# Thirty arrangements of the same products in the up-projection of a feed-forward block

## The chip, the core and the metric

The kernel runs on one core of one Trainium2 chip. The metric is the device time of one execution in microseconds; the time of a kernel is the median of several executions on the same chip.

## The reference

One layer of a decoder works on 272 tokens (16 meta tokens and 256 of the sequence) of width 2048. First comes a sparse attention beside a causal pooling, then a feed-forward part. Only the feed-forward part matters here:

```python
def conv_gated_ffn(h, w_up, conv_w, conv_b, w_down):
    T = h.shape[1]
    z = h @ w_up
    zp = jnp.pad(z, ((0, 0), (CONV_WIDTH - 1, 0), (0, 0)))
    z = sum(zp[:, j:j + T] * conv_w[j] for j in range(CONV_WIDTH)) + conv_b
    a, g = jnp.split(z, 2, axis=-1)
    return (jax.nn.gelu(a) * g) @ w_down
```

The inner width is 5632 for each of `a` and `g`. Everything is float32.

## The kernel before, in words

**Two parts per number.** Each float32 operand x of a large product is split into an upper part (x rounded to the format that TensorE multiplies in one pass, fp32r) and a lower part (x minus the upper part). A product of W and A is then three matmuls: upper W by upper A, upper W by lower A, lower W by upper A. `product` (lines 196 to 204) writes them in this order for each of the 16 row tiles k of the contraction (2048 = 16 x 128), so a block of 128 output channels is 48 matmuls that accumulate in one PSUM tile `mm`. The weights are the stationary operand (128 columns), the activations the moving one (258 columns: the 256 tokens and the two before them that the convolution needs). In the trace these are the lines 202, 203 and 204 with `mm<-hp,whl`.

**Weights.** `fetch` (lines 148 to 163) brings a weight tile of 128 x 2048 from HBM on the queue of SP into `wraw`; ScalarE (ACT) then writes the upper part (line 162) and VectorE (DVE) the lower part (line 163), each in two halves of 1024 columns, into the tile `whl`. There are three buffers of each, and the weights are fetched two blocks ahead. `whl` is a little longer than two parts need (4224 words a partition), and a table `spots` sets at which byte offsets the two parts begin: (0, 80) for the up-projection, where the second figure counts from 8192 bytes. The activations `hp` lie in slots of 576 words, the upper part from word 6, the lower one from word 270.

**The order of work.** `ffn_plan` writes the feed-forward part out as a list. The 44 tiles of the inner width are cut into parts of 8, 8, 8, 8, 8 and 4. Each of the 44 has two up blocks (for `a` and `g`), which makes 88. While the up blocks of one part are computed, the down-projection of the part before it is threaded between them, one weight tile after one up block. The first part, 16 up blocks, has no down-projection beside it; the other 72 up blocks have one.

**The down-projection** uses a Strassen-like scheme with seven products instead of eight: `forms` makes sums of the gated activations on GpSimd (POOL) and splits them into upper and lower parts (tiles `gp` and `right`), and `seven` (lines 770 to 793) runs for each weight tile four products (kind A), three (kind B) or, in one place, eight (kind C). Here the gated activations are stationary, and the weights move, 512 columns at a time: lines 791, 792, 793 with `at<-whl,gp` or `at<-whl,right`. In the program order of TensorE an up block of 48 matmuls is followed by 12 or 9 of the down-projection (24 for kind C).

After an up block, ACT and DVE apply the convolution, `gate` the two halves, and the result goes to `forms`. [...]

Of the kernel before, what the change touches and what calls it, by code (L numbers as in the profile page):

```python
# [17 lines left out]
P = 128  # L18
# [5 lines left out]
NQ = T - Q0  # L24
KT = D // P
# [9 lines left out]
PARTS = (8, 8, 8, 8, 8, 4)  # L35
# [37 lines left out]
def places(a, b):  # L73


    return a // 4, (8192 + (b if b >= a else b + 256)) // 4


def ffn_plan():

    plan, f0 = [], 0
    for part, n in enumerate(PARTS):
        ups = [("up", f, half_) for f in range(f0, f0 + n) for half_ in range(2)]
        downs = []
        if part:
            downs = [(kind, part - 1, c, j) for c in range(2) if (part - 1, c) != PLAIN for kind in "AB"
                     for j in range(PARTS[part - 1] // 2)]
        u, d = len(ups), len(downs)
        while ups or downs:
            if ups and (len(downs) * u <= len(ups) * d or not downs):  # L90
                plan.append(ups.pop(0))
            else:
                plan.append(downs.pop(0))
        f0 += n
    return plan + [("C", *PLAIN, j) for j in range(PARTS[PLAIN[0]] // 2)]
# [3 lines left out]
def tile_layer(ctx, tc, xt, w_first, w_proj, w_uk, w_uv, w_pool, w_o, w_up, w_down, cols, rows, rel_bias, onehot, out):  # L99
    nc = tc.nc  # L100
# [21 lines left out]
    ps = small()  # L122
# [4 lines left out]
    stream = [w_proj[j] for j in range(8)] + [w_uk, w_uv] + [w_proj[j] for j in range(8, 24)]  # L127
    stream += [w_o[j] for j in range(KT)]
    plan = ffn_plan()
    kinds, spots = {}, {}  # L130
    for i in range(8):
        spots[i], spots[10 + i], spots[18 + i] = ACROSS, QUERIES[i % 2], POOLED[i]
    for i in range(26, len(stream)):
# [1 line left out]
    for item in plan:  # L135
        if item[0] == "up":
            spots[len(stream)] = ACROSS
            stream.append(w_up[item[2] * FT + item[1]])
        else:
            kinds[len(stream)] = item[0]  # L140
            stream.append(w_down[sum(PARTS[:item[1]]) + item[2] * (PARTS[item[1]] // 2) + item[3]])
# [20 lines left out]
            nc.scalar.activation(hl[:, 0, c], raw[:, c], AF.Copy)  # L162
            nc.vector.tensor_tensor(hl[:, 1, c], raw[:, c], hl[:, 0, c].bitcast(F32), op=ALU.subtract)  # L163

    def weight_tiles(places):
        raw = wp.tile([P, 2048], F32, tag="wraw", name="wraw")
        t = wp.tile([P, WSLOT], F32R, tag="whl", name="whl")
        u, l = places
        return raw, Pair(t[:, u:u + 2048], t[:, l:l + 2048])

    def emit(i):
        if i in ready:
            return
        if i == spare:
            raw = wp.tile([P, 2048], F32, tag="wraw", name="wraw")
            hl = sb.tile([P, 2, 2048], F32R, tag="y", name="whl_y")
        else:
            raw, hl = weight_tiles(places(*spots.get(i, (0, 0))))
        fetch(raw, hl, stream[i], kinds.get(i))
        if i >= len(stream) - PARTS[-1]:  # L180
            k = i - len(stream) + PARTS[-1]
            nc.scalar.activation(raw[:, LAST:], raw[:, LAST:], AF.Copy, accum_out=wsums[:, k:k + 1])
        ready[i] = hl
# [6 lines left out]
    def weights(ahead=2):  # L190
        i = state["use"]
        state["use"] += 1
        prefetch(i + 1 + ahead)
        return ready.pop(i)

    def product(ps, hl, m, act, lo, hi, ks=range(KT), width=P, k0=0, k1=KT):

        for n in range(k0, k1):
            k = ks[n]
            wh, wl = hl[:, 0, k * width:k * width + m], hl[:, 1, k * width:k * width + m]  # L200
            ah, al = act[k][:, 0, lo:hi], act[k][:, 1, lo:hi]
            nc.tensor.matmul(ps, wh, ah, start=n == 0, stop=False)  # L202
            nc.tensor.matmul(ps, wh, al, start=False, stop=False)  # L203
            nc.tensor.matmul(ps, wl, ah, start=False, stop=n == KT - 1)  # L204
# [536 lines left out]
    def two_parts(a, src):  # L741
        nc.scalar.activation(a[:, 0], src, AF.Copy)
        nc.vector.tensor_tensor(a[:, 1], src, a[:, 0].bitcast(F32), op=ALU.subtract)
        return a

    def slot():
        a = fp.tile([P, 2, NE], F32R, name="gp", tag="gp", bufs=19)
        return a[:, :, :2 * P].rearrange("p a (b c) -> p a b c", c=P)

    def forms(p, r, j):

        a11, a21, a12, a22 = r[:, 0, :P], r[:, 0, P:], r[:, 1, :P], r[:, 1, P:]
        s = fp.tile([P, 4 * P], F32, name="forms", bufs=1).rearrange("p (a b) -> p a b", b=P)
        nc.gpsimd.tensor_tensor(s[:, 0], a21, a22, op=ALU.add)
        nc.gpsimd.tensor_tensor(s[:, 2], s[:, 0], a11, op=ALU.subtract)
        nc.gpsimd.tensor_tensor(s[:, 1], a12, s[:, 2], op=ALU.subtract)
        nc.gpsimd.tensor_tensor(s[:, 3], a11, a21, op=ALU.subtract)  # L759
        left = two_parts(slot(), r[:, :, :P])  # L760
        mid = two_parts(slot(), s[:, :2])
        right = ring.tile([P, SLOT], F32R, tag="act", name="right")
        right = Pair(*(right[:, o:o + 2 * P].rearrange("p (b c) -> p b c", c=P) for o in (0, T)))
        right = two_parts(right, s[:, 2:])
        if p == PLAIN[0]:
            lone, i = two_parts(slot(), r[:, :, P:]), 1
        else:
            if j % 2 == 0:
                held["lone"] = slot()
            lone, i = held["lone"], j % 2  # L770
            two_parts(lone[:, :, i], a22)
        return {"P1": (left, 0), "P2": (left, 1), "P5": (mid, 0), "P3": (mid, 1), "P6": (right, 0),
                "P7": (right, 1), "P4": (lone, i), "a21": (lone, 0)}

    def seven(kind, part, c, j):

        hl = weights()
        n = PARTS[part] // 2
        names = {"A": (("P2", 2), ("P3", 3), ("P1", 0), ("P5", 1)), "B": (("P7", 1), ("P6", 0), ("P4", 2)),
                 "C": (("P1", 0, "c11"), ("P2", 2, "c11"), ("P1", 1, "c12"), ("P2", 3, "c12"),  # L780
                       ("a21", 0, "c21"), ("P4", 2, "c21"), ("a21", 1, "c22"), ("P4", 3, "c22"))}[kind]
        done = []
        for name, w, *to in names:
            a, i = pairs[part][j][name]
            to = (to or [name])[0]
            fresh, last = j == 0 and to not in done, j == n - 1 and (kind != "C" or to in done)
            if fresh:
                held[to] = small()
            done.append(to)
            ps, w = held[to], slice(512 * w, 512 * w + 512)  # L790
            nc.tensor.matmul(ps, a[:, 0, i], hl[:, 0, w], start=fresh, stop=False)  # L791
            nc.tensor.matmul(ps, a[:, 0, i], hl[:, 1, w], start=False, stop=False)  # L792
            nc.tensor.matmul(ps, a[:, 1, i], hl[:, 0, w], start=False, stop=last)  # L793
        if j < n - 1:
            return
        c11, c12, c21, c22 = (y2[:, i, w:w + 512] for i in range(2) for w in (512 * c, 1024 + 512 * c))

        def add(to, ps):
            nc.vector.scalar_tensor_tensor(to, to, 1.0 if part else ALPHA, ps, op0=ALU.mult, op1=ALU.add)  # L799

        if kind == "C":
            for to, name in ((c11, "c11"), (c12, "c12"), (c21, "c21"), (c22, "c22")):
                add(to, held[name])
        elif kind == "A":
            held["u"] = fp.tile([P, 512], F32, name="u", tag="u1", bufs=1, padded_shape=[P, 2 * NQ])
            nc.scalar.activation(held["u"], held["P1"], AF.Copy)
            held["v"] = fp.tile([P, 512], F32, name="v", tag="u2", bufs=1, padded_shape=[P, 2 * NQ])
            nc.scalar.activation(held["v"], held["P5"], AF.Copy)
            add(c11, held["P2"])
            add(c12, held["P3"])  # L810
            nc.gpsimd.dma_start(c11, held["u"], accum_op=ALU.add)
            nc.gpsimd.dma_start(c12, held["v"], accum_op=ALU.add)
        else:
            u, v = held["u"], held["v"]
            add(c22, v)
            nc.vector.tensor_tensor(u, u, held["P6"], op=ALU.add)
            nc.vector.tensor_tensor(v, u, held["P7"], op=ALU.add)
            add(c21, held["P4"])
            nc.gpsimd.dma_start(c12, u, accum_op=ALU.add)
            nc.gpsimd.dma_start(c21, v, accum_op=ALU.add)  # L820
            nc.gpsimd.dma_start(c22, v, accum_op=ALU.add)
# [4 lines left out]
    for item in plan:  # L826
# [5 lines left out]
        if half_ == 0:  # L832
            if f % 2 == 0:
                pair = fp.tile([P, 2, S], F32, name="za", tag="z0", bufs=3)
            both = []
        hl = weights()
        ps = big()
        if todo and f > FOLDED - 1 + half_:
# [15 lines left out]
                continue  # L854
            both = [conv(i * FT + f, i, unfold(both[i]), pair[:, f % 2]) for i in range(2)]
        else:
            product(ps[:, :NQ], hl, P, h_parts, 0, NQ)
            both.append(conv(half_ * FT + f, half_, ps, pair[:, f % 2]))
            if half_ == 0:
                continue  # L860
# [190 lines left out]
```

## Time and profile before

| | |
|---|---|
| median of 3 runs | 1038.33 us (1038.06 to 1038.5) |
| the profiled execution, its own time | 1039.8 us |
| its span, first to last instruction | 1038.0 us |
| granted TensorE clock | 0.998 |
| TensorE (PE) busy | 1025.3 us, 99% of the span, 7649 matmuls |
| weight loads (PEld) busy | 973.8 us, 94% |
| DVE busy | 886.1 us, 85% |
| ACT busy | 617.4 us, 59% |
| POOL busy | 209.3 us, 20% |
| moved by DMA | 250.80 MB, mean 242 GB/s |

The profiled execution lies 1.5 us above the median of the runs; 1.8 us of its time lie outside the span. A row of a group names the line of the kernel, the engine, the operation, the tile written and those read, the shape and the count; behind the bar stand the busy time in us, the mean length of one in ns, and how long the engine was idle just before them. A row of the timeline has the start in us, the length in us, and the same names. Matmuls are pipelined, so that the length of one (0.28 us for 258 columns) is more than twice the distance between the starts of two; what a matmul costs is that distance.

### The profile page before, as it was taken

What the parts mean: (1) busy time and instruction counts of PE and PEld (TensorE: products, weight loads), DVE (VectorE), ACT (ScalarE), POOL (GpSimd) and SP (SyncE); (2) the same over time, 40 slices, a digit from 0 to 9 for tenths busy, and PEclk for the clock granted to TensorE, in tenths of its full rate; (3) what the DMA queues carried; (4) which work ended last, traced back from release to release, by engine and by line L of the source; (5) the groups of instructions that cost most, each with busy time, mean ns of one, the idle gap of its engine ahead of it and who ended that gap; (6) DMA issues with size and microseconds to landing.
All of it is one profiled execution on the core that took longest, in us unless ns stands there. A gap on an engine that the chain in (4) does not pass through costs nothing.

```text
span 1038.0 us, 19165 instructions
## 1 busy us (share of the span) xinstructions
PE 1025.3 (99%) x7649; PEld 973.8 (94%) x7649; DVE 886.1 (85%) x1372; ACT 617.4 (59%) x994; POOL 209.3 (20%) x262
## 2 busy tenths in 40 slices
PE   9999999999999999999999999999999999999996
PEld 8998999999999999998999999999999999999985
DVE  6879468758779997898999999899998998999866
ACT  7566356645447765565566655656555656566654
POOL 1100014125345311211122011120111201110022
PEclk9999999999999999999999999999999999999999
DMA  9766543454552587898798787887878878898766
GB/s 326 259 216 236 194 156 109 152 188 167 191 196 85 200 233 248 261 301 257 260 299 293 283 283 271 287 284 274 286 269 288 276 277 278 269 306 274 277 203 152
DMA packets 59610, 250.80 MB, mean 242 GB/s; under 512 B 21718, under 2 KB 22400, under 8 KB 32384
## 3 DMA queue, kind: packets, MB, share of 16 engines
q1 hardware_dynamic: 34016, 229.37, 61.5%
q0 software_dynamic: 8320, 17.71, 8.9%
q10 hardware_dynamic: 17184, 2.49, 1.4%
q8 instruction: 60, 0.98, 0.4%
q14 instruction: 30, 0.25, 0.1%
HBM read 233.55 MB, written 3.16 MB: 228 GB/s over the span
## 4 chain that ended last, share of the span: by engine, by line
PE 82%; DVE 7%; issue 5%; DMA 4%; POOL 1%; ACT 1%; DVEq 0%; POOLq 0%; ACTq 0%
PE mm L204 20%; PE mm L203 20%; PE mm L202 20%; PE at L792 5%; PE at L793 5%; PE at L791 5%; DVE whl L163 3%; DMA wraw<-in_w_down 2%; DMA wraw<-in_w_up 1%; DMA y<-x 1%; DVE x L704 1%; ACT whl L162 1%; DVE hp L708 1%; PE mm L265 1%; PE mm L267 1%
## 5 line engine op out<-in xcount | busy, mean ns | idle before, releaser
L163 DVE TENSOR_TENSOR whl<-wraw,whl 128x1024 fp32r<-128x1024 f32 (+1 forms) x418 | 492.7, 1213 | 53.8 <-ACT whl L162 52.9
L162 ACT ACTIVATE whl<-wraw 128x1024 fp32r<-128x1024 f32 (+1 forms) x418 | 405.0, 1014 | 147.4 <-DVE wraw L158 39.6
L204 PE MATMUL mm<-hp,whl 128*128 128x258 f32 x1280 | 360.8, 282 | 0.0
L203 PE MATMUL mm<-hp,whl 128*128 128x258 f32 x1280 | 359.7, 281 | 0.0
L202 PE MATMUL mm<-hp,whl 128*128 128x258 f32 x1280 | 355.5, 278 | 0.0
L202 PEld LDWEIGHTS mm<-hp,whl 128*128 128x128 f32 x1280 | 240.7, 188 | 3.1
L203 PEld LDWEIGHTS mm<-hp,whl 128*128 128x128 f32 x1280 | 239.6, 187 | 3.0
L204 PEld LDWEIGHTS mm<-hp,whl 128*128 128x128 f32 x1280 | 240.2, 188 | 0.0
L202 PE MATMUL mm<-xp,whl 128*128 128x256 f32 (+5 forms) x384 | 110.9, 289 | 0.0
L203 PE MATMUL mm<-xp,whl 128*128 128x256 f32 (+5 forms) x384 | 108.5, 282 | 0.0
L204 PE MATMUL mm<-xp,whl 128*128 128x256 f32 (+5 forms) x384 | 108.1, 282 | 0.0
L791 PE MATMUL at<-whl,gp 128*128 128x512 f32 x212 | 83.8, 395 | 0.9 <-DVE y L799 0.9
L792 PE MATMUL at<-whl,gp 128*128 128x512 f32 x212 | 83.8, 395 | 0.1
L793 PE MATMUL at<-whl,gp 128*128 128x512 f32 x212 | 83.4, 394 | 0.0
L203 PEld LDWEIGHTS mm<-xp,whl 128*128 128x128 f32 x384 | 72.3, 188 | 0.8 <-issue 0.5
L202 PEld LDWEIGHTS mm<-xp,whl 128*128 128x128 f32 x384 | 72.2, 188 | 0.6
L204 PEld LDWEIGHTS mm<-xp,whl 128*128 128x128 f32 x384 | 72.2, 188 | 0.3 <-DVE whl L163 0.2
L759 POOL TENSOR_TENSOR forms<-za 128x128 f32<-128x128 f32 x20 | 20.2, 1011 | 226.6 <-DVE za L739 212.1
L721 ACT ACTIVATE z<-mm,cv 128x256 f32<-128x256 f32 x40 | 22.5, 564 | 71.1 <-PE mm L204 70.2
L791 PEld LDWEIGHTS at<-whl,gp 128*128 128x128 f32 x212 | 39.8, 188 | 9.5 <-DVE y L799 1.4
L793 PEld LDWEIGHTS at<-whl,gp 128*128 128x128 f32 x212 | 39.8, 188 | 9.3
L721 ACT ACTIVATE za<-mm,cv 128x256 f32<-128x256 f32 x40 | 22.4, 560 | 43.6 <-PE mm L204 43.6
(316 smaller groups left out, 1854.6 us busy)
## 6 DMA issues: line engine op xcount, KB each, us to landing
wraw<-in_w_up SPq DMA_DIRECT2D x88, 1024.0 KB, 5.1
wraw<-in_w_down SPq DMA_DIRECT2D x80, 1024.0 KB, 6.8
wraw<-in_w_proj SPq DMA_DIRECT2D x24, 1024.0 KB, 5.1
wraw<-in_w_o SPq DMA_DIRECT2D x16, 1024.0 KB, 4.9
y<-v POOLq DMA_DIRECT2D x27, 256.0 KB, 8.5
y<-u POOLq DMA_DIRECT2D x18, 256.0 KB, 4.8
wraw<-in_w_first SPq DMA_DIRECT2D x8, 304.0 KB, 5.4
x<-in_xt SPq DMA_DIRECT2D x1, 2176.0 KB, 8.4
```

Of the source, the lines that this page charges most:

```text
L162: nc.scalar.activation(hl[:, 0, c], raw[:, c], AF.Copy)
L163: nc.vector.tensor_tensor(hl[:, 1, c], raw[:, c], hl[:, 0, c].bitcast(F32), op=ALU.subtract)
L202: nc.tensor.matmul(ps, wh, ah, start=n == 0, stop=False)
L203: nc.tensor.matmul(ps, wh, al, start=False, stop=False)
L204: nc.tensor.matmul(ps, wl, ah, start=False, stop=n == KT - 1)
L265: nc.tensor.matmul(ps[:m, :T], wh, x_parts[k][:, 0, :], start=k == 0, stop=False)
L267: nc.tensor.matmul(ps[:m, :T], wl, x_parts[k][:, 0, :], start=False, stop=k == KT - 1)
L721: nc.scalar.activation(z, src[:, 2:NQ], AF.Identity, bias=col(C_B, j), scale=col(C_W, 3 * j + 2))
L759: nc.gpsimd.tensor_tensor(s[:, 3], a11, a21, op=ALU.subtract)
L791: nc.tensor.matmul(ps, a[:, 0, i], hl[:, 0, w], start=fresh, stop=False)
L792: nc.tensor.matmul(ps, a[:, 0, i], hl[:, 1, w], start=False, stop=False)
L793: nc.tensor.matmul(ps, a[:, 1, i], hl[:, 0, w], start=False, stop=last)
```

## The change

The 72 up blocks that lie behind the first part are numbered in order of the tile f (from f = 8) and of the half: the block's number is 2 (f - 8) + half, and it takes entry number mod 30 of a table of 30 arrangements. The first 16 up blocks stay as they are. The entries are:

- 0 and 1, plain: as before.
- 2 swapped, 3 snake, 4 ahead, 5 by two: other orders of the 48 matmuls of a block. With U and L for upper and lower, weights first: plain is UU, UL, LU; swapped is UU, LU, UL; ahead is LU, UU, UL; snake runs every second row tile in reverse; by two takes two row tiles together and alternates between them.
- 6 to 29: for eight offsets of the weights (0, 32, ... 224 bytes further) each: mixed, back, back mixed. Mixed means that upper and lower weights lie in turn, element by element, so ACT and DVE write every second word, and the weight load reads every second word. Back means that the moving operand is read from its last column to its first, and the PSUM tile written so too, which gives the same tile.

As 72 is twice 30 and 12 more, there are 6 plain blocks, 3 each of the entries 2 to 5, and 18 each of mixed, back and back mixed: 36 blocks with weights in turn, 36 with a moving operand read backwards, 66 that differ from before in some way.

Two more edits concern the down-projection. The stationary tiles `gp` of the parts 1 to 4 have upper and lower elements in turn for every second pair of tiles (`slot(p > 0 and j % 2)`), and the matmuls of the parts 2 and 3 read the weights and write the PSUM tile backwards. Each part of kind A and B has 2 x 4 x (4 + 3) x 3 = 168 matmuls, so 336 are turned round. Of kind A (and C) matmuls with a `gp` tile of an odd pair there are 48 in each of the parts 1 to 3 and 48 in part 4: 192 with a stationary tile of step 2.

```diff
+BLENDS = [("plain", 0)] * 2 + [(how, 0) for how in ("swapped", "snake", "ahead", "by two")] +     [(how, 32 * q) for q in range(8) for how in ("mixed", "back", "back mixed")]
+def blend(i):
+    return BLENDS[i % len(BLENDS)]
...
+            if item[1] >= PARTS[0]:
+                blends[len(stream)] = blend(2 * (item[1] - PARTS[0]) + item[2])
...
-    def weight_tiles(places):
+    def weight_tiles(places, mixed=None):
         raw = wp.tile([P, 2048], F32, tag="wraw", name="wraw")
         t = wp.tile([P, WSLOT], F32R, tag="whl", name="whl")
+        if mixed is not None:
+            t = t[:, mixed // 4:mixed // 4 + 4096].rearrange("p (c two) -> p two c", two=2)
+            return raw, Pair(t[:, 0], t[:, 1])
...
-    def product(ps, hl, m, act, lo, hi, ks=range(KT), width=P, k0=0, k1=KT):
+    def product(ps, hl, m, act, lo, hi, ks=range(KT), width=P, k0=0, k1=KT, how="plain"):
+        if how != "plain":
+            terms = []
+            for n in range(KT):
+                w = slice(n * width, n * width + m)
+                three = [(hl[:, 0, w], act[n][:, 0, lo:hi]), (hl[:, 0, w], act[n][:, 1, lo:hi]),
+                         (hl[:, 1, w], act[n][:, 0, lo:hi])]
...
+            if "back" in how:
+                terms, ps = [(w, a[:, ::-1]) for w, a in terms], ps[:, ::-1]
+            for n, (w, a) in enumerate(terms):
+                nc.tensor.matmul(ps, w, a, start=n == 0, stop=n == len(terms) - 1)
+            return
...
-            nc.tensor.matmul(ps, a[:, 0, i], hl[:, 0, w], start=fresh, stop=False)
-            nc.tensor.matmul(ps, a[:, 0, i], hl[:, 1, w], start=False, stop=False)
-            nc.tensor.matmul(ps, a[:, 1, i], hl[:, 0, w], start=False, stop=last)
+            back = slice(None, None, -1 if part in (2, 3) else 1)
+            ps, wh, wl = ps[:, back], hl[:, 0, w][:, back], hl[:, 1, w][:, back]
+            nc.tensor.matmul(ps, a[:, 0, i], wh, start=fresh, stop=False)
+            nc.tensor.matmul(ps, a[:, 0, i], wl, start=False, stop=False)
+            nc.tensor.matmul(ps, a[:, 1, i], wh, start=False, stop=last)
```

On TensorE the number of matmuls, their sizes and the order of the blocks stay. Only inside a block the terms move. The place is the block with the PSUM tile `mm_5490`, the first with the arrangement "by two"; `hp_3878`, `hp_3884` and `hp_3890` are the activations of the first row tiles, `whl_5386` the weights of the block. TensorE before:

```order
L793 MATMUL at_5479<-whl_5355,gp_4479 128x512
L202 MATMUL mm_5490<-hp_3878,whl_5386 128x258
L203 MATMUL mm_5490<-hp_3878,whl_5386 128x258
L204 MATMUL mm_5490<-hp_3878,whl_5386 128x258
L202 MATMUL mm_5490<-hp_3884,whl_5386 128x258
L203 MATMUL mm_5490<-hp_3884,whl_5386 128x258
L204 MATMUL mm_5490<-hp_3884,whl_5386 128x258
```

The same place of TensorE after the change:

```order
L835 MATMUL at_5479<-whl_5355,gp_4479 128x512
L232 MATMUL mm_5490<-hp_3878,whl_5386 128x258
L232 MATMUL mm_5490<-hp_3884,whl_5386 128x258
L232 MATMUL mm_5490<-hp_3878,whl_5386 128x258
L232 MATMUL mm_5490<-hp_3884,whl_5386 128x258
L232 MATMUL mm_5490<-hp_3878,whl_5386 128x258
L232 MATMUL mm_5490<-hp_3884,whl_5386 128x258
L232 MATMUL mm_5490<-hp_3890,whl_5386 128x258
```

The matmul of the down-projection ahead of the block is the same one; in the block the two row tiles now alternate. In the other arrangements of order the three terms of a row tile change places among themselves.

The second place is the block with the tile `mm_5654`, the first that is read backwards. TensorE before:

```order
L793 MATMUL at_5479<-whl_5551,gp_4771 128x512
L202 MATMUL mm_5654<-hp_3878,whl_5570 128x258
L203 MATMUL mm_5654<-hp_3878,whl_5570 128x258
L204 MATMUL mm_5654<-hp_3878,whl_5570 128x258
L202 MATMUL mm_5654<-hp_3884,whl_5570 128x258
```

The same place of TensorE after the change (x3 stands for three matmuls with the same names):

```order
L835 MATMUL at_5479<-whl_5551,gp_4771 128x512
L232 MATMUL mm_5654<-hp_3878,whl_5570 128x258 x3
L232 MATMUL mm_5654<-hp_3884,whl_5570 128x258 x3
L232 MATMUL mm_5654<-hp_3890,whl_5570 128x258 x3
L232 MATMUL mm_5654<-hp_3952,whl_5570 128x258 x3
L232 MATMUL mm_5654<-hp_3958,whl_5570 128x258 x3
```

Nothing has moved here but the line number; what differs is the step of the moving operand and of the PSUM tile, which these rows do not show. On DVE, ACT, POOL and SP every instruction stands where it stood, with the same names and sizes; in blocks with weights in turn, the step of what ACT writes and DVE reads and writes is two words.

More of the change, by code (lines that the diff above doesn't have):

```diff
@@ L129, in tile_layer @@
     plan = ffn_plan()
-    kinds, spots = {}, {}
+    kinds, spots, blends = {}, {}, {}
     for i in range(8):
@@ L177, in emit @@
         else:
-            raw, hl = weight_tiles(places(*spots.get(i, (0, 0))))
+            how, at_ = blends.get(i, ("plain", 0))
+            spot = spots.get(i, (0, 0))
+            raw, hl = weight_tiles(places(spot[0] + at_, spot[1] + at_), at_ if "mixed" in how else None)
         fetch(raw, hl, stream[i], kinds.get(i))
@@ L194, in weights @@
         return ready.pop(i)
-    def product(ps, hl, m, act, lo, hi, ks=range(KT), width=P, k0=0, k1=KT):
+    def product(ps, hl, m, act, lo, hi, ks=range(KT), width=P, k0=0, k1=KT, how="plain"):
[5 more added lines that the diff above has]
+                         (hl[:, 1, w], act[n][:, 0, lo:hi])]
+                if how == "swapped":
+                    three = [three[i] for i in (0, 2, 1)]
+                if how == "ahead":
+                    three = [three[i] for i in (2, 0, 1)]
+                if how == "snake" and n % 2:
+                    three = three[::-1]
+                terms.append(three)
+            if how == "by two":
+                terms = [[terms[n + i][t] for t in range(3) for i in range(2)] for n in range(0, KT, 2)]
+            terms = [t for three in terms for t in three]
+            if "back" in how:
[3 more added lines that the diff above has]
+            return
         for n in range(k0, k1):
@@ L744, in two_parts, with slot @@
         return a
-    def slot():
+    def slot(mixed=False):
         a = fp.tile([P, 2, NE], F32R, name="gp", tag="gp", bufs=19)
+        if mixed:
+            a = a.rearrange("p a b -> p (a b)")[:, :4 * P]
+            return a.rearrange("p (b c a) -> p a b c", a=2, c=P)
         return a[:, :, :2 * P].rearrange("p a (b c) -> p a b c", c=P)
@@ L759, in forms @@
         nc.gpsimd.tensor_tensor(s[:, 3], a11, a21, op=ALU.subtract)
-        left = two_parts(slot(), r[:, :, :P])
-        mid = two_parts(slot(), s[:, :2])
+        left = two_parts(slot(p > 0 and j % 2), r[:, :, :P])
+        mid = two_parts(slot(p > 0 and j % 2), s[:, :2])
         right = ring.tile([P, SLOT], F32R, tag="act", name="right")
@@ L835, in tile_layer @@
             both = []
+        how = blends.get(state["use"], ("plain", 0))[0]
         hl = weights()
@@ L856, in tile_layer @@
         else:
-            product(ps[:, :NQ], hl, P, h_parts, 0, NQ)
+            product(ps[:, :NQ], hl, P, h_parts, 0, NQ, how=how)
             both.append(conv(half_ * FT + f, half_, ps, pair[:, f % 2]))
```

## The prediction

> **What bounds the kernel now.** The page comes first, its busy time by engine and the chain of work that ended last.
>
> ```profile
> PE 1025.3 (99%) x7649; PEld 973.8 (94%) x7649; DVE 886.1 (85%) x1372; ACT 617.4 (59%) x994; POOL 209.3 (20%) x262
> PE 82%; DVE 7%; issue 5%; DMA 4%; POOL 1%; ACT 1%; DVEq 0%; POOLq 0%; ACTq 0%
> ```
>
> TensorE is busy 99% of the span and carries 82% of the chain. Matmuls overlap, so busy time alone doesn't show a bound. I therefore read busy time by stretch over the whole time in which changed blocks run (from 406.38 us, when the first up block stands between two groups of the down-projection, to 980.5 us), the last stretch and the sum, and then who kept TensorE waiting between 403 and 981 us.
>
> ```profile
> 923.50:980.50 57.00, 57.00 (x413) 53.72 (x412) 51.82 (x71) 33.14 (x44) 2.77 (x4) 1.00 0.86 289
> sum 574.12, PE 573.13 PEld 540.10 DVE 527.96 ACT 344.23 POOL 92.61; mean PE 114.63 PEld 108.02 DVE 105.59 ACT 68.85 POOL 18.52
> PE at L791 <- DVE y L799: 0.9, 1, 0.9
> ```
>
> In 574.12 us of this stage TensorE is idle for 1.0 us, and 0.9 of that is one wait for DVE. The granted clock is 1.00. So the stage lasts as long as its matmuls need at the distance at which they follow each other, and the change acts on that distance alone, unless it makes another engine late. DVE has 574.12 - 527.96 = 46.2 us to spare, ACT 230 us.
>
> The distance is read from the timeline of TensorE, at the first instruction of each block: a group of the down-projection at 608.09, an up block at 610.88, the next group at 616.54, the next up block at 619.33.
>
> ```profile
> 608.09 0.39 PE L791 MATMUL at<-whl,gp 128*128 128x512 f32 x1
> 610.88 0.28 PE L202 MATMUL mm<-hp,whl 128*128 128x258 f32 x1
> 616.54 0.39 PE L791 MATMUL at<-whl,gp 128*128 128x512 f32 x1
> 619.33 0.28 PE L202 MATMUL mm<-hp,whl 128*128 128x258 f32 x1
> ```
>
> The 48 matmuls of the up block take 616.54 - 610.88 = 5.66 us, 117.9 ns each for 258 columns; the 12 of the down-projection take 2.79 us, 232.5 ns each for 512 columns. One more column therefore costs (232.5 - 117.9) / 254 = 0.451 ns. Nearly all of a matmul is the streaming of its columns.
>
> **The change part by part.** 66 of 72 up blocks differ, 66 x 48 = 3168 matmuls. Twelve of them only order the terms otherwise; 54, or 2592 matmuls, have weights of step 2, a moving operand and a PSUM tile of step -1, or both. No instruction is added on any engine, no DMA, no wait; nothing is moved past another queue. One nanosecond more or less per matmul on the 3168 is worth 3.2 us.
>
> *Order of terms and offset of the weights (one answer).* Other places of the weights are in the trace already, in the query projections, whose moving operand has 258 columns too. Their blocks begin, again in TensorE's timeline, at
>
> ```profile
> 100.01 0.28 PE L202 MATMUL mm<-xp,whl 128*128 128x258 f32 x1
> 105.77 0.28 PE L202 MATMUL mm<-xp,whl 128*128 128x258 f32 x1
> 122.75 0.28 PE L202 MATMUL mm<-xp,whl 128*128 128x258 f32 x1
> 128.40 0.28 PE L202 MATMUL mm<-xp,whl 128*128 128x258 f32 x1
> 315.79 0.29 PE L202 MATMUL mm<-fold,whl 128*128 128x260 f32 x1
> 321.57 0.28 PE L202 MATMUL mm<-fold,whl 128*128 128x260 f32 x1
> ```
>
> The block at 122.75 takes 5.65 us (117.7 ns a matmul), the one at 100.01 takes 5.76 us (120.0 ns). Both have the same offsets, (160, 224), so what differs is the work beside them; I keep 120.0 as the largest distance without a wait. The block at 315.79 has activations `fold` in slots of 520 words, so that their offsets differ from tile to tile; it takes 5.78 us, 120.4 ns for 260 columns, which is 119.5 ns after 0.9 ns for the two columns more. So other places give 117.7 to 120.0 ns, that is -0.2 to +2.1 ns against 117.9. A gain beyond that is bounded by the best stretch per column that I find, 27 matmuls of 256 columns in the indexer's projections:
>
> ```profile
> 58.52 0.28 PE L202 MATMUL mm<-xp,whl 128*128 128x256 f32 x1
> 61.64 0.28 PE L362 MATMUL at<-kidx,qi 128*128 128x256 f32 x1
> ```
>
> 3.12 us / 27 = 115.6 ns, 0.451 ns a column, where the up block has 117.9 / 258 = 0.457. On 258 columns that is 1.4 ns less, and 3168 x 1.4 = 4.5 us the most that I grant as a gain; 3168 x 2.1 = 6.7 us is the loss at the other end. For the twelve blocks of order alone I take nothing, after the block at 122.75, which is nearest: same sizes, other places.
>
> *Reading backwards.* No matmul of the trace has a negative step, so it is bounded from both sides. The nearest rows are of DVE, where line 445 reads and writes the 416 columns of `bias` from the last to the first, and line 368 does the same operation forwards.
>
> ```profile
> L445 DVE SCALAR_TENSOR_TENSOR bias<-work,bias 128x416 f32<-128x416 f32 x8 | 4.1, 588 | 0.0
> L368 DVE SCALAR_TENSOR_TENSOR score<-rl,widx,score 128x272 f32<-128x272 f32 x16 | 8.0, 498 | 0.0
> L368 DVE SCALAR_TENSOR_TENSOR score<-rl,widx,score 128x144 f32<-128x144 f32 x16 | 5.8, 365 | 1.7 <-ACT rl L365 1.7
> ```
>
> Forwards, 128 columns more cost 133 ns, so 416 columns would be about 650 ns; backwards they take 588. The one engine that the trace shows going backwards pays nothing for it. A gain is not excluded either, and is bounded by the 4.5 us. At the other end each column would cost twice its 0.451 ns (that is a rival, below). I take it at the price of another place: backwards, the moving stream and the weight load pass over each other's addresses in another way.
>
> [...]
>
> *Weights in turn.* The weight load reads 128 columns at a step of 8 bytes instead of 4. How long the load itself takes, the rows of weight loads of two sizes from one source show:
>
> ```profile
> L424 PEld LDWEIGHTS at<-whl,ctp 128*128 128x128 f32 x8 | 1.5, 188 | 0.4
> L424 PEld LDWEIGHTS at<-whl,ctp 128*16 128x16 f32 x4 | 0.4, 94 | 0.4
> ```
>
> (188 - 94) / 112 = 0.84 ns a column, 107 ns for 128. That runs beside the matmul before it and fits into 117.9 ns with 10 ns to spare, so a load up to a tenth slower costs nothing, and beyond that each nanosecond goes into the distance. In the down-projection the same load has 232.5 ns, so the 192 matmuls with a stationary tile of step 2 are covered even if it doubles. I take no cost for the step itself.
>
> ACT and DVE write every second word in 36 blocks. ACT has the room named above. If strided writing is free on DVE, nothing changes; the other end is a rival.
>
> *The down-projection backwards.* 336 matmuls of 512 columns, 192 with the other stationary; at -1 to +1 ns each this is half a microsecond, and I set it at nothing.
>
> *The sum.* For the 2592 matmuls of mixed and back I take 118.5 ns, +0.6, about midway between the 117.7 of the block at 122.75 and the 119.5 of `fold`, since neither is nearer to a stream of another step: 2592 x 0.6 = 1.6 us. Against the profiled execution this is 1039.8 + 1.6 = 1041.4; that execution lies 1.5 us over the median of the runs, 1038.33, so the median to come is 1039.9, say **1040 us**. The ends: 1038.33 - 4.5 - 0.5 = 1033.3 and 1038.33 + 6.7 + 0.5 = 1045.5. What is late next if the matmuls go faster: DVE, whose 46.2 us of room cover more than ten times the largest gain.
>
> **The rivals.** *Backward streams at half rate (slower, by much).* If descending columns are read or written one by one where ascending ones go in pairs, each column costs 0.90 ns: 36 x 48 = 1728 matmuls of 258 columns, 1728 x 258 x 0.451 = 201 us, and 336 x 512 x 0.451 = 78 us in the down-projection, together 1317 us. It is all or nothing from the first column. For it: no matmul of the trace goes that way. Against it: the DVE rows.
>
> *Weight loads that outlast the matmul (slower).* If a step of two words doubles the load to 215 ns, the distance in the 36 blocks with weights in turn is 215 instead of 117.9 ns: 1728 x 97 = 168 us, 1206 us. It decides from a load slower by a tenth. [...] No row of the trace has a strided load.
>
> *DVE as the bound (slower).* The rows of the split, 1024 and 512 columns:
>
> ```profile
> L163 DVE TENSOR_TENSOR whl<-wraw,whl 128x1024 fp32r<-128x1024 f32 x382 | 470.9, 1262 | 53.8 <-ACT whl L162 52.9
> L163 DVE TENSOR_TENSOR whl<-wraw,whl 128x512 fp32r<-128x512 f32 x36 | 24.9, 692 | 0.0
> ```
>
> 570 ns for 512 columns. If strided operands double that, 36 blocks x 2 x 1.14 = 82 us come to DVE, of which 46 fit: 36 us of waits of TensorE, 1074 us. It decides once an instruction takes over 46.2 / 72 = 0.64 us more, half as much again.
>
> *A gain.* If the distance over a column's own time is lost where weight load and moving stream meet in SBUF, streams that run at the same step in bytes (weights in turn) or against each other (back) may meet less often: up to 4.5 us, 1034 us. For it: the three matmuls of a row tile start at unequal distances, 0.11, 0.12 and 0.12 us, so what is read matters:
>
> ```profile
> 611.95 0.28 PE L202 MATMUL mm<-hp,whl 128*128 128x258 f32 x1
> 612.06 0.28 PE L203 MATMUL mm<-hp,whl 128*128 128x258 f32 x1
> 612.18 0.28 PE L204 MATMUL mm<-hp,whl 128*128 128x258 f32 x1
> 612.30 0.28 PE L202 MATMUL mm<-hp,whl 128*128 128x258 f32 x1
> ```
>
> Against it: the up blocks and the query block at 122.75, with different places, come to the same 117.7 and 117.9 ns on average, as if something else held the pace.
>
> *The change does nothing to the pace.* This is the same argument taken to the end: 1038.3 us. It is inside my forecast's case.
>
> **How the numbers follow.** A measurement of this kernel can tell about 0.2%, 2.1 us, from no change. The case without a structural price, 1033 to 1046, gets 0.78: faster by over 0.2% 0.18, within it 0.36, slower 0.24. Backward at half rate 0.13, weight loads 0.05, DVE 0.04. In all: faster 0.18, within 0.36, slower 0.46. The likeliest is the first case, with 1040. The range goes from 1032 to 1074: it takes in the first case with a little below it, and DVE; the two rivals left out above it hold 0.18, and at most 0.02 of the first case lies below it.
>
> **What would show it.** In the profile after, TensorE's timeline gives the length of every up block: 5.63 to 5.76 us in all of them proves the first case. Blocks near 11 us wherever the moving operand goes backwards prove the first rival, near 10.3 us wherever the weights lie in turn the second, and waits of TensorE for line 163 (174 in the changed kernel) with instructions well over 1262 ns the third. Groups of the down-projection should stay at 2.75 to 2.82 us for 12 matmuls. The prediction is wrong if any arrangement moves a block by more than 2%, or if the plain blocks move too.

## The result and the profile after

The changed kernel takes 1048.32 us (median of 3 runs, 1048.12 to 1048.37) against 1038.33: a ratio of 1.0096, 95% interval 1.0073 to 1.0119. It is slower by 10.0 us. The profiled execution of the changed kernel took 1048.12 us, its span 1046.3.

The page after, in the lines that answer to those of before (busy time by engine, chain, the groups of the changed matmuls and of the weight loads that changed and that did not):

```profile
PE 1033.6 (99%) x7649; PEld 983.3 (94%) x7649; DVE 886.9 (85%) x1372; ACT 626.9 (60%) x994; POOL 209.9 (20%) x262
PE 89%; DVE 4%; issue 4%; POOL 1%; DMA 1%; ACT 1%; SPq 0%; DVEq 0%; POOLq 0%; ACTq 0%
L232 PEld LDWEIGHTS mm<-hp,whl 128*128 128x128 f32 x3168 | 391.8, 193 | 5.6
L232 PE MATMUL mm<-hp,whl 128*128 128x258 f32 x3168 | 393.1, 283 | 0.0
L241 PEld LDWEIGHTS mm<-xp,whl 128*128 128x128 f32 x384 | 72.2, 188 | 0.3 <-DVE whl L174 0.2
```

TensorE is the bound as before; its busy time rose by 8.3 us, as the span did. ACT is busy 9.5 us longer too, at 60% of the span. In line 232, where the changed blocks are, a weight load lasts 193 ns on average instead of 188, while the unchanged ones of line 241 keep their 188. (The experiments below tell the arrangements apart.) The stage, from the same two events as in the prediction, now reads, in busy time by stretch:

```profile
406.88:988.92 582.04, 582.04 (x4145) 550.14 (x4143) 529.34 (x721) 354.33 (x475) 92.19 (x106) 1.00 0.83 277
```

It lasts 582.04 us instead of 574.19 (406.38 to 980.57), TensorE is busy for all of it, and no row is left in the view of what it waited for. The clock is 1.00. So the time went into the distance from matmul to matmul. TensorE's timeline at five up blocks and at the group behind each shows it: the second plain block, snake, and mixed, back and back mixed at offset 0 (x48 is a whole block in one row).

```profile
406.88 0.28 PE L239 MATMUL mm<-hp,whl 128*128 128x258 f32 x1
412.54 0.39 PE L833 MATMUL at<-whl,gp 128*128 128x512 f32 x1
...
423.76 5.88 PE L232 MATMUL mm<-hp,whl 128*128 128x258 f32 x48
429.48 0.40 PE L833 MATMUL at<-whl,gp 128*128 128x512 f32 x1
...
447.82 6.03 PE L232 MATMUL mm<-hp,whl 128*128 128x258 f32 x48
453.69 0.39 PE L833 MATMUL at<-whl,right 128*128 128x512 f32 x1
455.78 5.93 PE L232 MATMUL mm<-hp,whl 128*128 128x258 f32 x48
461.55 0.40 PE L833 MATMUL at<-whl,right 128*128 128x512 f32 x1
463.65 6.03 PE L232 MATMUL mm<-hp,whl 128*128 128x258 f32 x48
469.51 0.40 PE L833 MATMUL at<-whl,gp 128*128 128x512 f32 x1
```

The time of a block is the start of the group behind it minus its own start: 5.66 us for the plain one (117.9 ns a matmul, as before), 5.72 for snake (119.2), 5.87, 5.77 and 5.86 for the three others (122.3, 120.2, 122.1). All 72 blocks read in this way give, in ns a matmul:

| arrangement | blocks | mean | least | most |
|---|---|---|---|---|
| plain | 6 | 118.0 | 117.8 | 118.1 |
| swapped | 3 | 117.9 | 117.8 | 117.9 |
| snake | 3 | 119.3 | 119.2 | 119.4 |
| ahead | 3 | 118.0 | 117.9 | 118.1 |
| by two | 3 | 119.1 | 118.9 | 119.3 |
| mixed | 18 | 120.9 | 120.0 | 122.2 |
| back | 18 | 121.2 | 120.0 | 122.2 |
| back mixed | 18 | 121.4 | 120.7 | 122.2 |

The sum: mixed and back, in their three forms, cost 3.15 ns more on average, 2592 x 3.15 = 8.2 us; snake and by two 144 x (1.3 + 1.1) = 0.35 us; the groups of the down-projection are together 1.0 us longer in the parts 1 to 4. That is 9.5 of the 10.0 us. The spans differ by less (8.3 us), because the profiled execution of before held a wait near 468 us (the 0.9 us for DVE) that the one after lacks: its group is 1.2 us longer than there, and a block and a group soon after it are together 0.5 us longer than their like.

### The profile page after: what moved, and what is told of

It reads as the page before. It is cut to its first block, busy times and chain, and to the rows that moved or that the text cites. A ratio compares the mean times of both kernels' runs of the same rounds, so it can differ in the third digit from the quotient of the medians.

```text
span 1046.3 us, 19161 instructions
## 1 busy us (share of the span) xinstructions
PE 1033.6 (99%) x7649; PEld 983.3 (94%) x7649; DVE 886.9 (85%) x1372; ACT 626.9 (60%) x994; POOL 209.9 (20%) x262
## 4 chain that ended last, share of the span: by engine, by line
PE 89%; DVE 4%; issue 4%; POOL 1%; DMA 1%; ACT 1%; SPq 0%; DVEq 0%; POOLq 0%; ACTq 0%
PE mm L232 36%; PE mm L241 10%; PE mm L240 10%; PE mm L239 10%; PE at L833 5%; PE at L835 5%; PE at L834 5%; DVE whl L174 1%; DVE x L741 1%; DVE hp L745 1%; PE mm L304 1%; PE mm L302 1%; PE mm L303 1%; DMA wraw<-in_w_down 0%; PE at L399 0%
## 5 line engine op out<-in xcount | busy, mean ns | idle before, releaser
L173 ACT ACTIVATE whl<-wraw 128x1024 fp32r<-128x1024 f32 (+1 forms) x418 | 413.8, 1038 | 98.0 <-DVE wraw L169 24.1
L232 PEld LDWEIGHTS mm<-hp,whl 128*128 128x128 f32 x3168 | 391.8, 193 | 5.6
L232 PE MATMUL mm<-hp,whl 128*128 128x258 f32 x3168 | 393.1, 283 | 0.0
L241 PE MATMUL mm<-hp,whl 128*128 128x258 f32 x224 | 63.2, 282 | 0.0
L240 PE MATMUL mm<-hp,whl 128*128 128x258 f32 x224 | 62.9, 281 | 0.0
L239 PE MATMUL mm<-hp,whl 128*128 128x258 f32 x224 | 62.1, 277 | 0.0
L835 PEld LDWEIGHTS at<-whl,gp 128*128 128x128 f32 x212 | 40.3, 190 | 9.1
L833 PEld LDWEIGHTS at<-whl,gp 128*128 128x128 f32 x212 | 40.3, 190 | 7.9 <-DVE u L858 0.4
L834 PEld LDWEIGHTS at<-whl,gp 128*128 128x128 f32 x212 | 40.3, 190 | 7.9 <-DVE whl L174 0.4
```

Of the source, the lines that this page charges most:

```text
L232: nc.tensor.matmul(ps, w, a, start=n == 0, stop=n == len(terms) - 1)
L833: nc.tensor.matmul(ps, a[:, 0, i], wh, start=fresh, stop=False)
L834: nc.tensor.matmul(ps, a[:, 0, i], wl, start=False, stop=False)
L835: nc.tensor.matmul(ps, a[:, 1, i], wh, start=False, stop=last)
```

## The experiments

In all of them the down-projection is that of the kernel before, but for down_only. Most of the runs are one execution each and serve for their block times; a block time is the mean distance of its 48 matmuls, and one run measures a whole table. How well a block time repeats is said under plain_offsets.

**plain_offsets.** Step, direction and order as before, the place of the weights alone varied.

```diff
+BLENDS = [("plain", 32 * q) for q in range(8)]
```

> All 72 up blocks plain (order, step and direction as before), the weights 0, 32, ... 224 bytes further in turn; the down-projection as before. Theory A (alignment: a block's length depends on where the weights lie against the moving operand, step and direction cost nothing themselves): lengths spread between 5.65 and 5.87 us, the same offset giving the same length within 0.02 us each time; 5.66 at offset 0. Theory B (steps: step 2 and step -1 cost 2 to 4 ns a matmul themselves, offsets matter little): 5.66 us at all eight offsets, 1038.3 us. Theory C (offsets alone: any move of the weights away from (0, 80) costs, wherever the moving operand lies): 5.66 at offset 0 and about 5.80 at the other seven, about 1047 us.

TensorE's timeline at a block with offset 0 and the next one with offset 32:

```profile
464.05 0.28 PE L239 MATMUL mm<-hp,whl 128*128 128x258 f32 x1
469.72 0.39 PE L833 MATMUL at<-whl,gp 128*128 128x512 f32 x1
472.49 0.28 PE L239 MATMUL mm<-hp,whl 128*128 128x258 f32 x1
478.22 0.39 PE L833 MATMUL at<-whl,gp 128*128 128x512 f32 x1
```

5.67 and 5.73 us, 118.1 and 119.4 ns. The middle values of the nine blocks at each of the offsets 0 to 224 are 118.1, 119.5, 121.1, 118.9, 119.9, 120.5, 120.8 and 119.8 ns, the execution took 1044.7 us. B is out: the place alone moves a plain block by up to 3 ns.

But the place does not fix the length of a block for good. Two blocks with offset 64 in the same run:

```profile
742.72 0.29 PE L239 MATMUL mm<-hp,whl 128*128 128x258 f32 x1
748.54 0.39 PE L833 MATMUL at<-whl,gp 128*128 128x512 f32 x1
...
808.26 0.29 PE L239 MATMUL mm<-hp,whl 128*128 128x258 f32 x1
813.92 0.39 PE L833 MATMUL at<-whl,gp 128*128 128x512 f32 x1
```

The first takes 5.82 us (121.2 ns), the second 5.66 (117.9), and both keep a rhythm of three matmuls almost from their start: about 120, 121 and 123 ns in turn in the first, about 117, 116 and 121 in the second. At five of the eight offsets here the nine blocks spread by more than 0.5 ns; in the tables of 32 places below that is so at 1 place of plain_fine, 3 of back_fine, 6 of mixed_fine, none of back_mixed_fine, 3 of step_load and 9 of lower_moved. It is not chance: plain_fine and back_write, two executions, agree in every one of their 72 blocks within 0.03 ns. What decides which rhythm a block falls into was not tested.

**hp_shifted.** The same, and the moving operand 32 bytes further.

```diff
-        a = act_tile("hp", NQ)
+        t = ring.tile([P, SLOT], F32R, tag="act", name="hp")
+        a = Pair(t[:, 14:14 + NQ], t[:, 278:278 + NQ])
```

> As plain_offsets, and the moving operand hp lies 32 bytes further in its slots (words 14 and 278 instead of 6 and 270). A: the eight lengths of plain_offsets move on by one place, so that 5.66 us is now found at offset 32 and the length of offset 224 there at offset 0 here. B: 5.66 us at all. C: the same eight lengths as in plain_offsets.

The same two offsets, 0 and 32, in TensorE's timeline:

```profile
464.64 0.28 PE L239 MATMUL mm<-hp,whl 128*128 128x258 f32 x1
470.41 0.39 PE L834 MATMUL at<-whl,gp 128*128 128x512 f32 x1
473.18 0.28 PE L239 MATMUL mm<-hp,whl 128*128 128x258 f32 x1
478.86 0.39 PE L834 MATMUL at<-whl,gp 128*128 128x512 f32 x1
```

Now offset 0 takes 5.77 us (120.2 ns) and offset 32 takes 5.68 (118.3). The series is 119.9, 118.1, 119.4, 120.6, 120.0, 119.0, 120.2, 120.8. In six of the eight places it is that of plain_offsets moved on by one place, to 0.5 ns, with the last of it (119.8) now at the head. Two places are off by about 1 ns, 120.0 for 118.9 and 119.0 for 119.9; there plain_offsets has blocks of both lengths. C is out. What counts in the main is where the weights lie against the moving operand. That it repeats after 256 bytes rests on the one pair 119.8 and 119.9, and on the rhythm inside a block, which holds although the two operands move against each other by multiples of 256 bytes from row tile to row tile (row tiles of the weights are 512 bytes apart, slots of `hp` 2304).

**all_back_mixed_224.** One arrangement in all 72 blocks.

```diff
+BLENDS = [("back mixed", 224)]
```

> All 72 up blocks back mixed at offset 224, the one of the 24 new arrangements whose blocks took 5.67 us; the down-projection as before. A: 5.67 us in every block, 1038.3 + 72 x 0.01 = 1039 us, no difference to be measured. B: the 5.67 us were an accident of their neighbours; with step 2 and step -1 everywhere 5.80 us, 1038.3 + 72 x 0.14 = 1048 us.

Here the expectation stood on a misreading: I had numbered the blocks of the changed kernel from the first that stands behind a group of the down-projection, which is the second of the 72, and so took a plain block for "back mixed, 224". With the right number that arrangement has 120.8 ns (5.80 us) there too; the table above is by the right numbers. In this run a block near 564 us:

```profile
564.24 5.96 PE L232 MATMUL mm<-hp,whl 128*128 128x258 f32 x48
570.03 0.40 PE L833 MATMUL at<-whl,right 128*128 128x512 f32 x1
```

5.79 us; by the unrounded starts all 72 blocks take 120.7 to 120.9 ns. The time is 1049.22 us, ratio 1.0092 (1.0063 to 1.0121). From 2.8 ns over the plain block 3456 x 2.8 = 9.7 us follow, and 10.5 were measured. So the block times told the time of this kernel to 0.8 us. And theory A, that step and direction cost nothing, had lost its only evidence; the four runs behind down_only test it.

**down_only.** The two edits of the down-projection alone.

```diff
+BLENDS = [("plain", 0)]
```

> Up blocks all plain, the two edits of the down-projection alone. A: groups as in the changed kernel, 0.02 us longer where turned round: 1038.3 + 1 = 1039.3 us, and 5.66 us in every up block. B: the 336 turned matmuls and the 192 with step 2 cost 2 to 4 ns each, 1039.5 to 1040.4 us. If more than 2 us appear here, my reading that the up blocks hold the loss is wrong.

1039.49 us, ratio 1.0005 (0.9992 to 1.0017): no difference that can be measured. An up block of it:

```profile
561.59 0.28 PE L239 MATMUL mm<-hp,whl 128*128 128x258 f32 x1
567.25 0.39 PE L833 MATMUL at<-whl,right 128*128 128x512 f32 x1
```

5.66 us. The groups are 0.7 us longer in sum over the parts 1 to 4, most of it in the two that are turned round. The loss lies in the up blocks.

**plain_fine, back_fine, mixed_fine, back_mixed_fine.** Each arrangement at 32 places, 8 bytes apart.

```diff
+BLENDS = [("plain", 8 * q) for q in range(32)]
```

(and "back", "mixed", "back mixed" in the three others)

> Up blocks plain, the weights 0, 8, 16, ... 248 bytes further in turn (32 places, each at least twice); the down-projection as before. The yardstick for the three runs beside it. Theory A (alignment alone; step and direction cost nothing): best place 117.6 to 118.0 ns a matmul, mean over the places 119.5 to 120.3, worst about 122. Theory D (alignment, and on top of it a cost of step 2 or step -1 at every place): the same here.

> As plain_fine, with the moving operand and the PSUM tile back to front in all 72 up blocks. A: another place is best, but as good, 117.6 to 118.3 ns, and the mean over the places is that of plain_fine within 0.4 ns. D: no place under 119.5 ns, and a mean of about 121, 1 ns over plain_fine (the eight places measured so far gave 120.2 to 122.2).

> As plain_fine, with upper and lower weights element by element in all 72 up blocks (both parts move together, 0 to 248 bytes). A: best place 117.6 to 118.3 ns, mean that of plain_fine within 0.4 ns. D: no place under 119.5 ns, mean about 121. Theory A for ACT and DVE: instructions 173 and 174 keep their 1.04 and 1.22 us for 1024 columns; with a cost of strided operands they get longer.

> As plain_fine, both back and mixed in all 72 up blocks. A: best place 117.6 to 118.3 ns, mean that of plain_fine within 0.4 ns. D: no place under 119.5 ns, mean 121 or, if the two costs add, 122.

| run | time, us | best place, ns | mean of 32 | worst place |
|---|---|---|---|---|
| plain_fine | 1045.96 | 117.9 | 119.7 | 121.9 |
| back_fine | 1049.32 | 120.0 | 121.0 | 123.8 |
| mixed_fine | 1049.84 | 119.9 | 121.0 | 122.2 |
| back_mixed_fine | 1051.53 | 120.7 | 121.3 | 123.2 |

Five of the 32 plain places have 118.3 ns or less; of the 96 others none is under 119.9. D is right: reading at another step or direction costs 1.3 to 1.6 ns on average and 2 to 3 at the best place, on top of what the place costs (for back this holds at the one distance between upper and lower weights that was tried). In back mixed 20 of 32 places, all from 96 bytes on, have the same 120.7 or 120.8: the place has ceased to matter there. One such block, at offset 224 of back_mixed_fine:

```profile
896.31 5.96 PE L232 MATMUL mm<-hp,whl 128*128 128x258 f32 x48
902.11 0.40 PE L833 MATMUL at<-whl,right 128*128 128x512 f32 x1
```

**back_read, back_write.** Back taken apart: only the moving operand is read backwards, or only PSUM is written backwards. In both the convolution reads the PSUM tile back to front, and the output is as before.

```diff
-                terms, ps = [(w, a[:, ::-1]) for w, a in terms], ps[:, ::-1]
+                terms = [(w, a[:, ::-1]) for w, a in terms]      (back_read)
+                ps = ps[:, ::-1]                                 (back_write)
...
+            src = ps[:, :NQ][:, ::-1] if f >= PARTS[0] else ps
```

> As back_fine, but only the moving operand is read back to front; the PSUM tile is written forwards, and ACT and DVE read it back to front in the convolution. Theory R (the cost of going backwards lies in reading the moving operand from SBUF): the 32 places as in back_fine, mean about 121.0 ns a matmul, none under 119.5. Theory W (it lies in writing PSUM): as in plain_fine, mean 119.7, best 117.8.

> As back_fine, but only the PSUM tile is written back to front; the moving operand is read forwards. R: as in plain_fine, mean 119.7 ns, best 117.8, place by place the same lengths. W: mean about 121.0, none under 119.5.

The block at the same place, offset 64, in the four kernels; TensorE's timeline of plain_fine:

```profile
727.10 0.28 PE L239 MATMUL mm<-hp,whl 128*128 128x258 f32 x1
732.76 0.39 PE L833 MATMUL at<-whl,gp 128*128 128x512 f32 x1
```

of back_fine:

```profile
728.66 6.02 PE L232 MATMUL mm<-hp,whl 128*128 128x258 f32 x48
734.51 0.40 PE L833 MATMUL at<-whl,gp 128*128 128x512 f32 x1
```

of back_read:

```profile
728.61 6.02 PE L232 MATMUL mm<-hp,whl 128*128 128x258 f32 x48
734.47 0.40 PE L833 MATMUL at<-whl,gp 128*128 128x512 f32 x1
```

of back_write:

```profile
725.83 5.82 PE L232 MATMUL mm<-hp,whl 128*128 128x258 f32 x48
731.49 0.39 PE L833 MATMUL at<-whl,gp 128*128 128x512 f32 x1
```

5.66, 5.85, 5.86 and 5.66 us, from starts rounded to 0.01 us. Over the 32 places back_read agrees with back_fine, and back_write with plain_fine, within 0.03 ns in every block by the unrounded starts; the executions took 1049.14 and 1044.53 us. R is right, W is out: writing PSUM backwards costs a matmul 0.03 ns at most, and the cost of back lies in the read of the moving operand.

**step_load.** The strided weight load without the strided writes; it takes other weights than the reference does, so the output is not the reference's.

```diff
-                w = slice(n * width, n * width + m)
+                k0 = min(n, KT - 2) * width
+                w = slice(k0, k0 + 2 * m, 2)
```

> Weights stored as before, one part behind the other, at 32 places; but each weight load reads every second column of two neighbouring row tiles, so the products are of other weights than the reference's. Theory L (the cost of mixed is in the strided load): mean about 121.0 ns a matmul as in mixed_fine, none under 119.5, and the writes of ACT at 1.05 us. Theory S (it is in the strided writes of ACT and DVE, which collide more with TensorE): as in plain_fine, mean 119.7, best 117.8.

Mean 121.2 ns, best 120.0, worst 122.1; 1050.22 us. L is right. The group of ACT's writes, first in step_load:

```profile
L173 ACT ACTIVATE whl<-wraw 128x1024 fp32r<-128x1024 f32 x382 | 386.9, 1052 | 118.0 <-DVE wraw L169 33.4 <-DMA wraw<-in_w_up 20.8 <-PE mm L242 20.7
```

then in mixed_fine:

```profile
L173 ACT ACTIVATE whl<-wraw 128x1024 fp32r<-128x1024 f32 x382 | 401.1, 1093 | 101.3 <-DVE wraw L169 25.0 <-PE mm L241 20.7 <-DVE wraw L165 17.6
L174 DVE TENSOR_TENSOR whl<-wraw,whl 128x1024 fp32r<-128x1024 f32 x382 | 470.8, 1263 | 51.0 <-ACT whl L173 49.4
```

The strided write costs ACT (1093 - 1052) x 382 / 144 = 109 ns on each of the 144 instructions of up blocks that do it, a tenth, for which ACT, busy for 60% of the span of the changed kernel, has room. (In the changed kernel the 72 instructions that do it last 1192 ns on average against 1052, by the unrounded lengths.) DVE pays nothing: 1263 ns, against 1262 before. So the cost of mixed is in the load. The weight loads themselves, first in the kernel before, then in step_load:

```profile
L202 PEld LDWEIGHTS mm<-hp,whl 128*128 128x128 f32 x1280 | 240.7, 188 | 3.1
L233 PEld LDWEIGHTS mm<-hp,whl 128*128 128x128 f32 x3456 | 429.4, 196 | 5.8
```

They last 196 ns in mixed_fine too, 197 in back_mixed_fine and 190 in the blocks of back of the changed kernel, where the load is unchanged. Step 2 makes the row of the load 8 ns longer and costs 1.5 ns a matmul over the 119.7 of plain_fine here.

**lower_moved.** A search for a place better than that of the kernel before: the lower weights alone moved.

```diff
-            raw, hl = weight_tiles(places(spot[0] + at_, spot[1] + at_), at_ if "mixed" in how else None)
+            raw, hl = weight_tiles(places(spot[0], spot[1] + at_), at_ if "mixed" in how else None)
```

> Plain, the upper weights at their place, the lower ones alone 0, 8, ... 248 bytes further. If 117.8 ns is a floor that several places reach (five of 32 in plain_fine): none under 117.6, between 117.8 and about 120. If the three terms add up freely (their means went from 114.0 to 125.2 in plain_fine): some place at 116 or 117, which would make a kernel faster than both.

Mean 119.2 ns, worst 122.0, best 117.7. A block at offset 176, one of the best:

```profile
839.69 0.28 PE L239 MATMUL mm<-hp,whl 128*128 128x258 f32 x1
845.34 0.40 PE L833 MATMUL at<-whl,right 128*128 128x512 f32 x1
```

5.65 us. Eight of 32 places have 118.3 ns or less on the mean of their blocks and none is under 117.7, so the terms do not add up freely: about 117.8 ns a matmul is a floor of the places tried, which many of them reach. The blocks of the kernel before have 118.05 on average; the best place lies 0.3 ns below, worth 1.2 us at most. The runs point to no version that clearly beats it.

## Why the prediction was right or wrong

**The bound.** Right: TensorE's distance from matmul to matmul decides, nothing else became late, and no wait was added.

**The rivals.** The large ones did not come: a block of back has 5.8 us and not 11, one of mixed 5.8 and not 10.3, DVE's instructions kept their length (1262 ns), and in the stage TensorE never waited for line 174. That ascending columns go in pairs, as the first rival supposed, no run shows; that a load of step 2 would hardly outlast the matmul was my estimate, without a row of such a load. The gain did not come either. It rested on the two read streams of TensorE meeting more or less often according to how they run; that the distance depends on where the two operands lie against each other is what plain_offsets and hp_shifted show, that the streams collide is not shown, and the sign was wrong: the other arrangements are slower.

**The sum.** The step that failed is the size of one term: "For the 2592 matmuls of mixed and back I take 118.5 ns, +0.6". It measured 121.2 ns, 3.15 over the plain blocks, and the time came out at 1048.3 instead of 1040. It was mis-sized in two ways. First, a place taken without fitting costs more than my two rows said: 119.7 ns is the mean over 32 places, 1.7 over the blocks of before (118.0), and the 120.0 ns that I kept as the largest distance is not even the worst plain place (121.9). The block at 122.75 us, which pulled my value down, stands on the floor of 117.8 itself. That the block at 100.01 us has the same offsets and yet 120.0 ns, I put down to the work beside it; no run shows that, and plain_offsets has blocks of one place that differ as much. Second, I took no price for step and direction, for the direction on the word of a row of DVE, for the step by an estimate; for TensorE they cost 1.3 to 1.6 ns more. The argument that a weight load up to a tenth slower is covered by the matmul beside it failed as well: 8 ns more in its row is less than the 10 ns I had to spare, and each matmul still paid 1.3 to 1.5 ns. Together 2592 x (1.7 + 1.4) = 8.0 us, of 8.2 measured. For order alone I took nothing: right for swapped and ahead, 1.1 to 1.3 ns too little for snake and by two, 0.35 us.

**The range.** The measured 1048.3 lies inside 1032 to 1074, but above the first case (1033 to 1046), and inside only because the range was drawn up to the price of the DVE rival, which is not what happened. By the sign that I named, blocks of 5.63 to 5.76 us in all, the first case was not fulfilled: most blocks of mixed and back took 5.76 to 5.87. The likeliest part of that case, a time within 0.2%, was wrong; slower by over 0.2%, with 0.46, was the right side, though 0.24 of it stood for losses inside the first case and 0.22 for the rivals, and neither came as told. That the range holds the result is luck. The sign of being wrong, a block moved by more than 2%, did come: the blocks of mixed and back have 120.0 to 122.2 ns against 118.0, 1.7 to 3.6% more.

**The down-projection.** Set at nothing; 0.7 to 1.0 us by the groups, too little to be seen in the time. The bound of 1 ns a matmul was too small all the same: in down_only the groups of the parts 2 and 3 are 0.6 us longer, 1.9 ns for each of the 336 matmuls turned round (96 of which have the other stationary tile too). A matmul of 512 columns leaves the weight load 232.5 ns instead of 117.9, and these paid no less than the 1.3 ns of back.

**What stays open.** Whether and why the pattern repeats after 256 bytes in full, why a read of step -1 or 2 has a higher floor, and whether another distance between upper and lower weights would bring back down to 117.8 ns was not tried or settled; that weight load and moving stream get into each other's way is a reading of the longer rows of the weight loads (190 ns for back, 196 for mixed, 188 before), not shown by itself. Open too is what sets the rhythm of a block, and so whether a faster rhythm of back or mixed exists that no block here fell into.

## What to carry to other kernels

Where TensorE is busy 99% of the time, price a change of operand layout in ns per matmul from the starts in its timeline, and take a number of places, not the best-looking one, as the price of an unfitted layout: this kernel, at 118.0 ns, stood 0.3 ns above the best place that lower_moved found, and the mean of the 32 places of plain_fine, 119.7 ns, lies 1.4% higher. A layout that differs from block to block turns one profiled execution into a table of dozens of measurements. Give each entry several blocks: most agree within 0.5 ns, but at some places they differ by 1 to 3 ns. Number the blocks from the program and not from the first one that stands out, and confirm the best entry by running it alone.

## What the runs showed of the hardware

- The distance between matmuls of 258 fp32r columns depends on the place of weights against moving operand within 256 bytes: 117.9 to 121.9 ns at 32 places 8 bytes apart (plain_fine). With both moved by 32 bytes, six of eight places stay within 0.5 ns and two differ by about 1 ns (hp_shifted).
- The same place can give two lengths, each with its own repeating rhythm of three matmuls: 117.9 and 121.2 ns at offset 64 of plain_offsets.
- A moving operand read from its last column to its first costs 1.3 ns on average (121.0 in back_fine against 119.7 in plain_fine), a PSUM tile written backwards 0.03 ns at most (back_write against plain_fine, block by block).
- A weight load of step 2 costs 1.3 to 1.5 ns on average per matmul of 258 columns, and its row is 196 ns long instead of 188 (step_load, mixed_fine).
- ACT writes every second word 10 to 14% slower (1052 ns for 1024 columns; about 1160 in mixed_fine, 1192 in the changed kernel, about 1200 in back_mixed_fine by the means of its rows), DVE at the same speed (1262 and 1263 ns).
- A matmul of fp32r operands is one row of TensorE (in the kernel before 1280 rows of line 202 for 80 blocks of 16), one of float32 operands two (16 rows of line 484 for 8 matmuls).
